# Instance normalisation on one core: units of 24 channels in 48 KB rows instead of 16 channels in 32 KB rows

## The chip, the cores and the metric

The kernel runs on one core of one Trainium2 chip. Times are device microseconds (us) of a whole run, and the metric is the median of several runs. A profile shows one execution; its span reaches from the first to the last instruction.

## The reference

The input x has shape 4 x 8 x 16 x 256 x 256 in 32-bit floats: 512 channels of 65,536 values, 134.2 MB. Each channel is normalised by itself and scaled by its gamma:

```python
mu = x.mean(axis=(3, 4), keepdims=True)
var = ((x - mu) ** 2).mean(axis=(3, 4), keepdims=True)
x_norm = (x - mu) / np.sqrt(var + 1e-5)
out = x_norm * gamma[None, :, :, None, None]
```

Gamma has 128 values and repeats for each of the four batches. Every value must be read once and written once: 268.4 MB over the memory.

## The kernel before, in words

Channels lie one after another in memory. The kernel takes them in 32 units of 16 channels. A unit is 4 MB and lies on 128 partitions with 8,192 floats (32 KB) in each, so a channel has exactly 8 whole partitions. Six slots in on-chip memory (`xt0` to `xt5`) hold six units, and unit u uses slot u mod 6.

Loads are issued ahead: the first six before the loop (units 1 and 3 on ScalarE's queue, the others on SyncE's), then, at the end of each turn of the loop, the load of unit u + 6 on SyncE's queue (L48 in `load`). That load must wait until the store of unit u has left the slot. All stores are issued by ScalarE (L139). Two small transfers go out from GpSimd at the start: `touch` (L54), a few zeros into the first unit of the output, written over later, and the gamma row (L55).

The loop runs over the 32 units. For one unit:

- VectorE sums each partition (L106), and ScalarE squares the same data and sums the squares (L107; the squares themselves go to `junk` and are not used). The two pairs of numbers stand in `st`.
- TensorE multiplies `st` with a constant matrix `navg` (L115) that adds the 8 partitions of each channel and spreads the sum back over the same 8 partitions, times minus one over 65,536. The result `ps` holds minus the mean and minus the mean square on every partition.
- VectorE forms minus the variance, `nvar` (L116), ScalarE takes the root (L120), VectorE the reciprocal (L124) and the product with gamma (L126).
- VectorE adds and multiplies the unit in place (L135). For unit 0 alone ScalarE does the last three eighths of each row (L132), with a `shift` from L131.
- ScalarE issues the store, and SyncE the load of unit u + 6.

The order on each engine is that of the program, since the schedule is written by hand (`manual_schedule`). Gamma is brought into columns before the loop: VectorE repeats it (L80), TensorE turns it into columns with eight products (L85), and VectorE copies them out (L91). An instruction of the loop that waits holds up all later ones of its engine: a store on ScalarE waits for the normalising, and the next squares stand behind it.

Of the kernel before, what the change touches and what calls it, by code (L numbers as in the profile page):

```python
# [1 line left out]

# [4 lines left out]

F32 = mybir.dt.float32
U8 = mybir.dt.uint8
ALU = mybir.AluOpType  # L10
ACTF = mybir.ActivationFunctionType
AX = mybir.AxisListType


@with_exitstack
def kernel(
    ctx: ExitStack,
    tc: tile.TileContext,
    x: bass.AP,
    gamma: bass.AP,  # L20
    out: bass.AP,
):
    nc = tc.nc
    B, G, C, H, W = x.shape
    P = nc.NUM_PARTITIONS
    HW = H * W
    n_ch = B * G * C
    S = 8
    K = P // S
    F = HW // S  # L30
    U = n_ch // K
    NG = (G * C) // K
    AHEAD = 6
    assert HW % S == 0 and (G * C) % K == 0

    xv = x.rearrange("b g c h w -> (b g c h w)").rearrange("(u p f) -> u p f", p=P, f=F)
    ov = out.rearrange("b g c h w -> (b g c h w)").rearrange("(u p f) -> u p f", p=P, f=F)
    gv = gamma.rearrange("g c -> (g c)")

    data = ctx.enter_context(tc.tile_pool(name="data", bufs=1))  # L40
    singles = ctx.enter_context(tc.tile_pool(name="singles", bufs=1))
    psum = ctx.enter_context(tc.tile_pool(name="psum", bufs=4, space=bass.MemoryType.PSUM))
    ctx.enter_context(tc.manual_schedule())

    slots = [data.tile([P, F], F32, name=f"xt{i}") for i in range(AHEAD)]

    def load(u, queue):
        queue.dma_start(out=slots[u % AHEAD][:], in_=xv[u])  # L48


    g_row = singles.tile([1, G * C], F32, name="g_row")
    touch = singles.tile([16, 128], F32, name="touch")
    nc.vector.memset(touch[:], 0.0)  # L53
    nc.gpsimd.dma_start(out=ov[0][0::S, 0:128], in_=touch[:])  # L54
# [8 lines left out]
    navg = singles.tile([P, K, S], F32, name="navg")  # L63
    nc.gpsimd.memset(navg[:], -1.0 / HW)  # L64
    nc.gpsimd.affine_select(  # L65
        out=navg[:], in_=navg[:], pattern=[[-S, K], [0, S]], compare_op=ALU.is_ge,
        fill=0.0, base=0, channel_multiplier=1,
    )
    nc.gpsimd.affine_select(  # L69
        out=navg[:], in_=navg[:], pattern=[[S, K], [0, S]], compare_op=ALU.is_ge,  # L70
        fill=0.0, base=S - 1, channel_multiplier=-1,
    )
    navg_w = navg[:].rearrange("p k s -> p (k s)")
    root_eps = singles.tile([P, 1], F32, name="root_eps")
    nc.scalar.activation(out=root_eps[:], in_=eps_t[:], func=ACTF.Sqrt)  # L75
    g_rep = singles.tile([1, NG, K, S], F32, name="g_rep")
    g_ps = psum.tile([P, NG], F32, name="g_ps", bufs=1)
    g_col = singles.tile([P, NG], F32, name="g_col")

    nc.vector.tensor_copy(  # L80
        out=g_rep[:],
        in_=g_row[:].rearrange("o (n k) -> o n k", n=NG).unsqueeze(3).to_broadcast([1, NG, K, S]),
    )
    for n in range(NG):
        nc.tensor.matmul(  # L85
            out=g_ps[:, n : n + 1],
            lhsT=g_rep[:, n].rearrange("o k s -> o (k s)"),
            rhs=one[:],
            start=True, stop=True,
        )  # L90
    nc.vector.tensor_copy(out=g_col[:], in_=g_ps[:])  # L91

    junk = singles.tile([P, F], U8, name="junk")

    st = singles.tile([P, U, 2], F32, name="st")
# [3 lines left out]
    scale = singles.tile([P, U], F32, name="scale")  # L99

    shift = singles.tile([P, 1], F32, name="shift")

    squares = []
    for u in range(U):
        t = slots[u % AHEAD]
        nc.vector.reduce_sum(out=st[:, u, 0:1], in_=t[:], axis=AX.X)  # L106
        square = nc.scalar.activation(  # L107
            out=junk[:], in_=t[:], func=ACTF.Square, accum_out=st[:, u, 1:2],
        )
        if u:  # L110

            tc.declare_no_dep(square.ins, squares[-1].ins, reason="junk, ordered by the root between")
        squares.append(square)
        ps = psum.tile([P, 2], F32, name="ps")
        nc.tensor.matmul(out=ps[:], lhsT=navg_w, rhs=st[:, u], start=True, stop=True)  # L115
        nc.vector.tensor_scalar(  # L116
            out=nvar[:, u : u + 1], in0=ps[:, 0:1], scalar1=ps[:, 0:1],
            scalar2=ps[:, 1:2], op0=ALU.mult, op1=ALU.add,
        )
        nc.scalar.activation(  # L120
            out=std[:, u : u + 1], in_=nvar[:, u : u + 1], func=ACTF.Sqrt,
            bias=eps_t[:], scale=-1.0,
        )
        nc.vector.reciprocal(out=rstd[:, u : u + 1], in_=std[:, u : u + 1])  # L124
        g = u % NG
        nc.vector.tensor_mul(  # L126
            out=scale[:, u : u + 1], in0=rstd[:, u : u + 1], in1=g_col[:, g : g + 1],
        )
        cut = F * 5 // 8 if u == 0 else F
        if cut < F:  # L130
            nc.vector.tensor_mul(out=shift[:], in0=ps[:, 0:1], in1=scale[:, u : u + 1])  # L131
            nc.scalar.activation(  # L132
                out=t[:, cut:], in_=t[:, cut:], func=ACTF.Identity, bias=shift[:], scale=scale[:, u : u + 1],
            )
        nc.vector.tensor_scalar(  # L135
            out=t[:, :cut], in0=t[:, :cut], scalar1=ps[:, 0:1], scalar2=scale[:, u : u + 1],
            op0=ALU.add, op1=ALU.mult,
        )
# [6 lines left out]
_INS = ['x', 'gamma']  # L145
_OUTS = [((4, 8, 16, 256, 256), 'float32')]


# [23 lines left out]
```

## Time and profile before

| what | value |
|---|---|
| median of 3 runs | 626.75 us (626.69 to 626.85) |
| span of the profiled execution | 625.2 us |
| busy: VectorE, ScalarE, TensorE | 441.8 us (71%), 241.8 (39%), 21.4 (3%) |
| mean DMA rate over the span | 429 GB/s |
| DMA packets | 9282, of them 8192 rows of 32 KB |
| SyncE's queue (q1), ScalarE's queue (q10) | 125.83 MB, 142.61 MB |
| memory read, written | 134.22 MB, 134.23 MB |
| time from issue to landing, median: stores, SyncE's loads | 62.5 us, 38.5 us |

The page gives no time of the profiled execution other than its span; the median of the runs is 1.5 us above it. In the tables of groups, a row has the line, the engine, the operation, what it writes and reads with shapes, the count, then the busy time in us and the mean of one in ns, and last the idle time of the engine just before these instructions with what ended it. The row of slices cuts the span into 40 equal parts; each digit is the busy share in tenths. "SPq" is SyncE's sequencer, which issues transfers and waits for semaphores. A time from issue to landing contains the time in which a transfer stands behind earlier ones of its queue.

### The profile page before, as it was taken

The numbers are of one execution on the slowest core, as the hardware profiler recorded it, in microseconds if no ns is written. First come the engines' busy times: TensorE is split into PE (matmuls) and PEld (weight loads), VectorE is DVE, ScalarE is ACT, GpSimd is POOL, SyncE is SP. The second block draws the span as 40 slices with busy tenths as digits, with TensorE's granted clock in tenths as the row PEclk, the third lists the DMA queues.
The fourth block names the chain that finished last, engine by engine and source line by source line (L and its number), as shares of the span: only waits on it lengthen the run. The fifth ranks groups of instructions, "written<-read, shape, count | busy, mean of one in ns | idle before, by whom it ended". The sixth has DMA issues, their size and how long they took to land.

```text
span 625.2 us, 635 instructions
## 1 busy us (share of the span) xinstructions
PE 21.4 (3%) x80; PEld 19.5 (3%) x80; DVE 441.8 (71%) x164; ACT 241.8 (39%) x99; POOL 2.4 (0%) x11
## 2 busy tenths in 40 slices
PE   0200000000000000000000000000000000000000
PEld 0200000000000000000000000000000000000000
DVE  0589999998776687666786767867668676687730
ACT  0464444444443244432344423444224442244400
POOL 1000000000000000000000000000000000000000
DMA  8999999999999999999999999999999999999998
GB/s 370 436 407 432 436 436 436 436 436 430 423 436 434 434 428 434 434 436 436 436 436 428 426 436 436 432 430 434 434 436 436 436 436 421 432 436 434 434 430 367
DMA packets 9282, 268.46 MB, mean 429 GB/s; under 512 B 1072, under 2 KB 1088, under 8 KB 1088
## 3 DMA queue, kind: packets, MB, share of 16 engines
q10 hardware_dynamic: 4896, 142.61, 52.9%
q1 hardware_dynamic: 4320, 125.83, 46.8%
q0 software_dynamic: 64, 0.01, 0.0%
q14 instruction: 2, 0.02, 0.0%
HBM read 134.22 MB, written 134.23 MB: 429 GB/s over the span
## 4 chain that ended last, share of the span: by engine, by line
another core or an unknown queue 61%; DMA 17%; DVE 15%; SPq 1%; PE 1%; issue 0%; ACT 0%
DMA xt<-in_x_dram 10%; DVE st L106 10%; DMA out_dram<-xt 8%; DVE xt L135 5%; SPq L48 1%; PE ps L115 1%; ACT std L120 0%; DVE nvar L116 0%; DVE rstd L124 0%; DVE scale L126 0%; DVE shift L131 0%
## 5 line engine op out<-in xcount | busy, mean ns | idle before, releaser
L106 DVE TENSOR_REDUCE st<-xt 128x1 f32<-128x8192 f32 x32 | 277.9, 8684 | 102.2 <-DMA xt<-in_x_dram 102.2
L107 ACT ACTIVATE junk<-xt 128x8192 uint8<-128x8192 f32 x32 | 225.0, 7030 | 272.0 <-DMA xt<-in_x_dram 233.8
L135 DVE TENSOR_SCALAR xt<-xt,ps,scale 128x8192 f32<-128x8192 f32 (+1 forms) x32 | 144.0, 4500 | 1.1
L120 ACT ACTIVATE std<-nvar,eps_t 128x1 f32<-128x1 f32 x32 | 9.4, 295 | 79.4 <-DVE nvar L116 79.4
L115 PE MATMUL ps<-st,navg 128*128 128x2 f32 x64 | 17.8, 348 | 557.3 <-DVE st L106 557.3
L115 PEld LDWEIGHTS ps<-st,navg 128*128 128x128 f32 x64 | 16.0, 310 | 559.1 <-issue 546.2
L116 DVE TENSOR_SCALAR nvar<-ps 128x1 f32<-128x1 f32 x32 | 9.2, 286 | 23.8 <-PE ps L115 23.8
L124 DVE RECIPROCAL rstd<-std 128x1 f32<-128x1 f32 x32 | 5.2, 163 | 11.6 <-ACT std L120 11.6
L80 DVE COPY g_rep<-g_row 1x1024 f32<-1x1024 f32 x1 | 0.7, 681 | 14.4 <-DMA g_row<-in_gamma_dram 14.4
L107 ACT ACTIVATION_READ_ACCUMULATOR junk<-xt 128x1 f32 x32 | 6.0, 186 | 0.0
L126 DVE TENSOR_TENSOR scale<-rstd,g_col 128x1 f32<-128x1 f32 x32 | 5.1, 158 | 1.1
L85 PE MATMUL g_ps<-one,g_rep 1*128 1x1 f32 x16 | 3.5, 347 | 16.3 <-DVE g_rep L80 16.3
L85 PEld LDWEIGHTS g_ps<-one,g_rep 1*128 1x128 f32 x16 | 3.5, 326 | 16.3 <-issue 16.3
L132 ACT ACTIVATE xt<-xt,shift,scale 128x3072 f32<-128x3072 f32 x1 | 2.9, 2947 | 0.7 <-DVE shift L131 0.7
L91 DVE COPY g_col<-g_ps 128x8 f32<-128x8 f32 x1 | 0.2, 167 | 3.7 <-PE g_ps L85 3.7
L75 ACT ACT_TABLE_LOAD x1 | 1.3, 1283 | 1.7 <-PEq L156 1.7
L53 DVE MEMSET touch<- 16x128 f32 x1 | 0.2, 165 | 0.9 <-PEq L156 0.9
L54 POOL DMA_DIRECT2D out_dram<-touch x1 | 0.6, 617 | 0.8 <-DVE touch L53 0.8
L55 POOL DMA_DIRECT2D g_row<-in_gamma_dram x1 | 0.5, 487 | 0.0
L65 POOL TENSOR_SCALAR_AFFINE_SELECT navg<-navg 128x128 f32<-128x128 f32 x1 | 0.4, 400 | 0.1
L69 POOL TENSOR_SCALAR_AFFINE_SELECT navg<-navg 128x128 f32<-128x128 f32 x1 | 0.4, 399 | 0.1
L64 POOL MEMSET navg<- 128x128 f32 x1 | 0.2, 230 | 0.0
(8 smaller groups left out, 1.0 us busy)
## 6 DMA issues: line engine op xcount, KB each, us to landing
out_dram<-xt ACTq DMA_DIRECT2D x32, 4096.0 KB, 62.5
xt<-in_x_dram SPq DMA_DIRECT2D x30, 4096.0 KB, 38.5
xt<-in_x_dram ACTq DMA_DIRECT2D x2, 4096.0 KB, 31.7
out_dram<-touch POOLq DMA_DIRECT2D x1, 8.0 KB, 9.3
g_row<-in_gamma_dram POOLq DMA_DIRECT2D x1, 0.5 KB, 13.5
```

The source lines that it names most:

```text
L48: queue.dma_start(out=slots[u % AHEAD][:], in_=xv[u])
L75: nc.scalar.activation(out=root_eps[:], in_=eps_t[:], func=ACTF.Sqrt)
L85: nc.tensor.matmul(out=g_ps[:, n : n + 1], lhsT=g_rep[:, n].rearrange("o k s -> o (k s)"), rhs=one[:], start=True, stop=True,)
L106: nc.vector.reduce_sum(out=st[:, u, 0:1], in_=t[:], axis=AX.X)
L107: square = nc.scalar.activation(out=junk[:], in_=t[:], func=ACTF.Square, accum_out=st[:, u, 1:2],)
L115: nc.tensor.matmul(out=ps[:], lhsT=navg_w, rhs=st[:, u], start=True, stop=True)
L116: nc.vector.tensor_scalar(out=nvar[:, u : u + 1], in0=ps[:, 0:1], scalar1=ps[:, 0:1], scalar2=ps[:, 1:2], op0=ALU.mult, op1=ALU.add,)
L120: nc.scalar.activation(out=std[:, u : u + 1], in_=nvar[:, u : u + 1], func=ACTF.Sqrt, bias=eps_t[:], scale=-1.0,)
L124: nc.vector.reciprocal(out=rstd[:, u : u + 1], in_=std[:, u : u + 1])
L126: nc.vector.tensor_mul(out=scale[:, u : u + 1], in0=rstd[:, u : u + 1], in1=g_col[:, g : g + 1],)
L132: nc.scalar.activation(out=t[:, cut:], in_=t[:, cut:], func=ACTF.Identity, bias=shift[:], scale=scale[:, u : u + 1],)
L135: nc.vector.tensor_scalar(out=t[:, :cut], in0=t[:, :cut], scalar1=ps[:, 0:1], scalar2=scale[:, u : u + 1], op0=ALU.add, op1=ALU.mult,)
```

## The change

The channels are cut into 20 units of 24 channels (6 MB, 12,288 floats or 48 KB in each partition) and, last, two units of 16 channels as before. Four slots of 48 KB a partition take the place of six of 32 KB. All loads are issued by SyncE, each as one transfer; `split` is empty. With 24 channels on 128 partitions, a channel is 16 pieces of 4,096 floats and a partition holds three pieces (j = 0, 1, 2), which can belong to two channels. So:

- the sum of a unit has three results a partition, and the squares are three instructions of 4,096;
- three products with `navg3` add up the pieces into one row for each of the 24 channels (`ps` on 24 partitions), and `nvar`, root, reciprocal and gamma are worked out on 24 partitions;
- minus the mean is copied beside the scale into `coef`, and three products with `spread` bring both back to 128 partitions, once for each piece (`wide`, in PSUM);
- VectorE normalises the three pieces one by one with both numbers read from `wide`. In units 0, 19, 20 and 21 (`helped`) ScalarE takes a part: the third piece of a 24-channel unit, or three eighths of a 16-channel one.

GpSimd makes three constant matrices instead of one. Gamma's columns come from 18 products instead of eight. `ps` and `wide` have two buffers each in PSUM, where `ps` had four.

```diff
-    S = 8
-    K = P // S
-    F = HW // S
-    U = n_ch // K
-    NG = (G * C) // K
-    AHEAD = 6
+    GC = G * C
+    F = 4096
+    SLOTS = 4
+    sizes = [2] * 0 + [3] * ((n_ch - 16 * 2) // 24) + [2] * 2
+    U = len(sizes)
+    starts = [sum(sizes[:i]) for i in range(U)]
+    split = {}
+    helped = (0, U - 3, U - 2, U - 1)
...
-    psum = ctx.enter_context(tc.tile_pool(name="psum", bufs=4, space=bass.MemoryType.PSUM))
+    psum = ctx.enter_context(tc.tile_pool(name="psum", bufs=2, space=bass.MemoryType.PSUM))
...
-    slots = [data.tile([P, F], F32, name=f"xt{i}") for i in range(AHEAD)]
-    def load(u, queue):
-        queue.dma_start(out=slots[u % AHEAD][:], in_=xv[u])
+    slots = [data.tile([P, 3 * F], F32, name=f"xt{i}") for i in range(SLOTS)]
+    def load(u):
+        cut = split.get(u, 0) * F
+        if cut:
+            nc.scalar.dma_start(out=home(u)[:, :cut], in_=rows(xf, u)[:, :cut])
+        if cut < sizes[u] * F:
+            nc.sync.dma_start(out=home(u)[:, cut:], in_=rows(xf, u)[:, cut:])
...
-    for u in range(AHEAD):
-        load(u, nc.scalar if u in (1, 3) else nc.sync)
+    for u in range(SLOTS):
+        load(u)
...
+    firsts = sorted({8 * starts[u] % GC for u in range(U) if sizes[u] == 3})
+    for n, c in enumerate(firsts):
+        nc.tensor.matmul(
+            out=g_ps3[:, n : n + 1], lhsT=g_two[:, c : c + K], rhs=one[:],
+            start=True, stop=True,
+        )
+    nc.vector.tensor_copy(out=g_col3[:], in_=g_ps3[:])
...
-        nc.vector.reduce_sum(out=st[:, u, 0:1], in_=t[:], axis=AX.X)
-        square = nc.scalar.activation(
-            out=junk[:], in_=t[:], func=ACTF.Square, accum_out=st[:, u, 1:2],
-        )
+        if three:
+            nc.vector.reduce_sum(
+                out=st[:, u, :, 0], in_=t.rearrange("p (j f) -> p j f", j=3), axis=AX.X,
+            )
...
+        step = F if three else cols
+        for j in range(cols // step):
+            square = nc.scalar.activation(
+                out=junk[:, :step], in_=t[:, j * step : (j + 1) * step],
+                func=ACTF.Square, accum_out=st[:, u, j, 1:2],
+            )
...
+            for j in range(3):
+                nc.tensor.matmul(
+                    out=ps[:n], lhsT=navg3[:, j], rhs=st[:, u, j], start=j == 0, stop=j == 2,
+                )
...
+        if three:
+            nc.vector.tensor_copy(out=coef[:n, u, 0:1], in_=ps[:n, 0:1])
...
+            for j in range(3):
+                nc.tensor.matmul(
+                    out=wide[:, j], lhsT=spread[:, j], rhs=coef[:n, u], start=True, stop=True,
+                )
+            mine = 2 if u in helped else 3
+            if u in helped:
+                own = singles.tile([P, 2], F32, name=f"own{u}")
+                nc.vector.tensor_copy(out=own[:, 1:2], in_=wide[:, 2, 1:2])
+                nc.vector.tensor_mul(out=own[:, 0:1], in0=wide[:, 2, 0:1], in1=own[:, 1:2])
+                nc.scalar.activation(
+                    out=t[:, 2 * F :], in_=t[:, 2 * F :], func=ACTF.Identity,
+                    bias=own[:, 0:1], scale=own[:, 1:2],
+                )
+            for j in range(mine):
+                nc.vector.tensor_scalar(
+                    out=t[:, j * F : (j + 1) * F], in0=t[:, j * F : (j + 1) * F],
+                    scalar1=wide[:, j, 0:1], scalar2=wide[:, j, 1:2], op0=ALU.add, op1=ALU.mult,
+                )
...
-        cut = F * 5 // 8 if u == 0 else F
+            cut = cols * 5 // 8 if u in helped else cols
...
-        nc.scalar.dma_start(out=ov[u], in_=t[:])
-        if u + AHEAD < U:
-            load(u + AHEAD, nc.sync)
+        nc.scalar.dma_start(out=rows(of, u), in_=t)
+        if u + SLOTS < U:
+            load(u + SLOTS)
```

More of the change, by code (lines that the diff above doesn't have):

```diff
@@ L38, with rows @@
+    U = len(sizes)
+    starts = [sum(sizes[:i]) for i in range(U)]
+    assert 8 * sum(sizes) == n_ch
+    split = {}
+    helped = (0, U - 3, U - 2, U - 1)
+    xf = x.rearrange("b g c h w -> (b g c h w)")
+    of = out.rearrange("b g c h w -> (b g c h w)")
     gv = gamma.rearrange("g c -> (g c)")
+    def rows(flat, u):
+        lo = starts[u] * P * F
+        return flat[lo : lo + sizes[u] * P * F].rearrange("(p f) -> p f", p=P)
     data = ctx.enter_context(tc.tile_pool(name="data", bufs=1))
@@ L52, with home @@
+    def home(u):
+        return slots[u % SLOTS][:, : sizes[u] * F]
+    def load(u):
[4 more added lines that the diff above has]
+            nc.sync.dma_start(out=home(u)[:, cut:], in_=rows(xf, u)[:, cut:])
+    g_row = singles.tile([1, GC], F32, name="g_row")
     touch = singles.tile([16, 128], F32, name="touch")
     nc.vector.memset(touch[:], 0.0)
-    nc.gpsimd.dma_start(out=ov[0][0::S, 0:128], in_=touch[:])
+    nc.gpsimd.dma_start(out=rows(of, 0)[0::8, 0:128], in_=touch[:])
@@ new lines @@
+    nc.gpsimd.affine_select(
+        out=navg3[:], in_=navg3[:], pattern=[[-1, 3], [16, K]], compare_op=ALU.is_ge,
+        fill=0.0, base=15, channel_multiplier=-3,
+    )
+    spread = singles.tile([K, 3, P], F32, name="spread")
+    nc.gpsimd.memset(spread[:], 1.0)
+    nc.gpsimd.affine_select(
+        out=spread[:], in_=spread[:], pattern=[[1, 3], [3, P]], compare_op=ALU.is_ge,
+        fill=0.0, base=0, channel_multiplier=-16,
+    )
+    nc.gpsimd.affine_select(
+        out=spread[:], in_=spread[:], pattern=[[-1, 3], [-3, P]], compare_op=ALU.is_ge,
+        fill=0.0, base=15, channel_multiplier=16,
+    )
@@ L74 @@
     root_eps = singles.tile([P, 1], F32, name="root_eps")
     nc.scalar.activation(out=root_eps[:], in_=eps_t[:], func=ACTF.Sqrt)
[L76 to L82, printed above, removed]
-    )
-    for n in range(NG):
+    g_two = singles.tile([1, GC + K], F32, name="g_two")
@@ new lines @@
+    nc.vector.tensor_copy(out=g_two[:, :GC], in_=g_row[:])
+    nc.vector.tensor_copy(out=g_two[:, GC:], in_=g_row[:, :K])
+    sixteens = sorted({8 * starts[u] % GC for u in range(U) if sizes[u] == 2})
+    g_rep = singles.tile([1, len(sixteens), 16, 8], F32, name="g_rep")
+    g_ps = psum.tile([P, len(sixteens)], F32, name="g_ps", bufs=1)
+    g_col = singles.tile([P, len(sixteens)], F32, name="g_col")
+    for n, c in enumerate(sixteens):
+        nc.vector.tensor_copy(
+            out=g_rep[:, n], in_=g_row[:, c : c + 16].unsqueeze(2).to_broadcast([1, 16, 8]),
+        )
@@ L85 @@
         nc.tensor.matmul(
-            out=g_ps[:, n : n + 1],
-            lhsT=g_rep[:, n].rearrange("o k s -> o (k s)"),
-            rhs=one[:],
+            out=g_ps[:, n : n + 1], lhsT=g_rep[:, n].rearrange("o k s -> o (k s)"), rhs=one[:],
             start=True, stop=True,
@@ L98 @@
     rstd = singles.tile([P, U], F32, name="rstd")
-    scale = singles.tile([P, U], F32, name="scale")
+    coef = singles.tile([P, U, 2], F32, name="coef")
     shift = singles.tile([P, 1], F32, name="shift")
@@ L104 @@
     for u in range(U):
-        t = slots[u % AHEAD]
-        nc.vector.reduce_sum(out=st[:, u, 0:1], in_=t[:], axis=AX.X)
-        square = nc.scalar.activation(
-            out=junk[:], in_=t[:], func=ACTF.Square, accum_out=st[:, u, 1:2],
[L109 to L113, printed above, removed]
-        ps = psum.tile([P, 2], F32, name="ps")
-        nc.tensor.matmul(out=ps[:], lhsT=navg_w, rhs=st[:, u], start=True, stop=True)
+        t = home(u)
@@ new lines @@
+        three = sizes[u] == 3
+        cols = sizes[u] * F
+        if three:
+            nc.vector.reduce_sum(
+                out=st[:, u, :, 0], in_=t.rearrange("p (j f) -> p j f", j=3), axis=AX.X,
+            )
+        else:
+            nc.vector.reduce_sum(out=st[:, u, 0, 0:1], in_=t, axis=AX.X)
+        step = F if three else cols
[3 more added lines that the diff above has]
+                func=ACTF.Square, accum_out=st[:, u, j, 1:2],
+            )
+            if squares and j == 0:
+                tc.declare_no_dep(square.ins, squares[-1].ins, reason="junk, ordered by the root between")
+            squares.append(square)
@@ L116 @@
+        n = K if three else P
+        ps = psum.tile([P, 2], F32, name="ps")
+        if three:
+            for j in range(3):
+                nc.tensor.matmul(
+                    out=ps[:n], lhsT=navg3[:, j], rhs=st[:, u, j], start=j == 0, stop=j == 2,
+                )
+        else:
+            nc.tensor.matmul(
+                out=ps[:], lhsT=navg2[:].rearrange("p k s -> p (k s)"), rhs=st[:, u, 0],
+                start=True, stop=True,
+            )
         nc.vector.tensor_scalar(
-            out=nvar[:, u : u + 1], in0=ps[:, 0:1], scalar1=ps[:, 0:1],
@@ L118 @@
-            scalar2=ps[:, 1:2], op0=ALU.mult, op1=ALU.add,
+            out=nvar[:n, u : u + 1], in0=ps[:n, 0:1], scalar1=ps[:n, 0:1],
+            scalar2=ps[:n, 1:2], op0=ALU.mult, op1=ALU.add,
         )
         nc.scalar.activation(
-            out=std[:, u : u + 1], in_=nvar[:, u : u + 1], func=ACTF.Sqrt,
-            bias=eps_t[:], scale=-1.0,
-        )
[L124 to L128, printed above, removed]
@@ L140 @@
-        if u + AHEAD < U:
-            load(u + AHEAD, nc.sync)
+            out=std[:n, u : u + 1], in_=nvar[:n, u : u + 1], func=ACTF.Sqrt,
+            bias=eps_t[:n], scale=-1.0,
+        )
+        if three:
+            nc.vector.tensor_copy(out=coef[:n, u, 0:1], in_=ps[:n, 0:1])
+        nc.vector.reciprocal(out=rstd[:n, u : u + 1], in_=std[:n, u : u + 1])
+        if three:
+            g = firsts.index(8 * starts[u] % GC)
+            gamma_u = g_col3[:, g : g + 1]
+        else:
+            g = sixteens.index(8 * starts[u] % GC)
+            gamma_u = g_col[:, g : g + 1]
```

55 lines of the change are left out of this document (34 added, 21 removed).

## The prediction

> **What bounds the kernel now.** I read the page's slices first, then its queues, its groups of instructions, the queue engine's waits and the chain of waits, and last the two ends of the span in half-microsecond windows. The slices, DMA share and rate:
>
> ```profile
> DMA  8999999999999999999999999999999999999998
> GB/s 370 436 407 432 436 436 436 436 436 430 423 436 434 434 428 434 434 436 436 436 436 428 426 436 436 432 430 434 434 436 436 436 436 421 432 436 434 434 430 367
> ```
>
> The 16 DMA engines are full in every slice but the first and last. No compute engine is (VectorE, the busiest, 71%):
>
> ```profile
> L106 DVE TENSOR_REDUCE st<-xt 128x1 f32<-128x8192 f32 x32 | 277.9, 8684 | 102.2 <-DMA xt<-in_x_dram 102.2
> L107 ACT ACTIVATE junk<-xt 128x8192 uint8<-128x8192 f32 x32 | 225.0, 7030 | 272.0 <-DMA xt<-in_x_dram 233.8
> L135 DVE TENSOR_SCALAR xt<-xt,ps,scale 128x8192 f32<-128x8192 f32 (+1 forms) x32 | 144.0, 4500 | 1.1
> ```
>
> The reduction and the squares wait for loads, never for each other for long. And loads wait for stores to leave a slot, as SyncE's own waits say:
>
> ```profile
> SPq L48 <- DMA out_dram<-xt: 514.7, 26, 39.7
> ```
>
> The chain of waits (start, length, what) gives the beat of one unit:
>
> ```profile
> 159.94 0.33 SPq L48
> ...
> 179.27 0.33 SPq L48
> ...
> 547.02 0.03 issue
> ```
>
> The load issued at 159.94 and the one issued at 547.05 (at the end of the last row) are 20 units apart: 387.1 / 20 = 19.356 us a unit, for one load and one store of 4.194 MB, 433.4 GB/s. Thirty-two units are 619.4. The rest of the span stands at its ends (last columns: DMA share, GB/s; a packet counts where it starts):
>
> ```profile
> 1.00:1.50 0.50, 0.00 (x0) 0.00 (x0) 0.06 (x1) 0.00 (x0) 0.14 (x1) 1.00 0.00 0
> 1.50:2.00 0.50, 0.00 (x0) 0.00 (x0) 0.00 (x0) 0.27 (x1) 0.50 (x2) 1.00 1.83 524
> ...
> 622.50:623.00 0.50, 0.00 (x0) 0.00 (x0) 0.00 (x0) 0.00 (x0) 0.00 (x0) 1.00 0.15 66
> 623.00:623.50 0.50, 0.00 (x0) 0.00 (x0) 0.00 (x0) 0.00 (x0) 0.00 (x0) 1.00 0.01 0
> ```
>
> In the trace's packet records the first row starts at 1.82 and the last ends at 623.93. So the span of 625.2 is 1.8 + 622.1 of DMA + 1.3. Of the 622.1, 619.4 is the beat and 2.7 irregular: the first packets took 1.25 to 2.01 us instead of 1.213 (0.65 lost), those around 41 us, where the first store joins, up to 2.01 (0.75), and the rest is small change and the engines' uneven finish. The median of the runs is 626.75, 1.5 over the span; I carry that 1.5 over.
>
> So only three things can move the time: what a packet costs beyond its bytes, when the engines have nothing to move, and the two ends.
>
> **Packets.** In the packet records a 512 B packet of touch took 27 ns and a 32 KB row 1213 ns: (32768 - 512) / (1213 - 27) = 27.2 bytes a ns. Sixteen rows (8 in, 8 out, per engine) are 16 x 32768 / 27.2 = 19.276 us; the beat of 19.356 leaves 0.080 us a unit for 16 packets and two 4-byte completions, 2.56 us in all. After: 40 transfers of 8 x 48 KB rows and four of 8 x 32 KB per engine, so 352 packets and 44 completions instead of 512 and 64. Both ratios are 0.6875: 2.56 becomes 1.76, **0.8 us saved**. If the residue is a clock and not a cost per packet, 0; if a 48 KB row goes out as three 16 KB packets (1024 of them), 2.56 more. I take 0.8: 512 B and 32 KB lie on one line whose intercept is some 8 ns, so the residue is per packet.
>
> **Head.** Before, SyncE and ScalarE's queue each issue loads at 0.81; after, SyncE alone issues four (before, its four issues took 0.38 to 0.61 us each and were done by 2.8). First packet at 1.82 as before. One 6 MB load alone is 8 x 1.81 = 14.5 us, so loads last until 1.8 + 0.65 + 58 = 60.5 if nothing joins. From here to the first store one queue is alone. Before never shows loads alone; both bounds come from rows: stores alone, after 604, ran 32 KB rows at the same 1.209 spacing (nothing lost), and the first packets, with nothing ahead, lost 0.65. Some 24 packets an engine at 0.65 would be 15.6 us. I take 0: the second packet of each engine in the head is already down to 1.21 to 1.27. The Trainium skill weighs both ways. Its page DMA: Bandwidth & Descriptors, section Issuing engines are not separate DMA queues, says all queues run on the same 16 engines, so a second one saves only issue time: by that, 0. But its section iDMA fabric gives 408.7 GB/s for one load stream from SP alone (4 KiB rows); an estimate from that figure over 44 us, against 433.4, is 2.7 us lost. No run here shows it yet.
>
> Then the store of unit 0 must be there before loads run out, and the store of unit 1 before store 0 ends. Unit 0: lands at 1.8 + 0.65 + 14.5 + 1.6 (the lag from last packet to reduction, 583.99 to 585.57) = 18.5. VectorE first waits for gamma: its row landed at 15.5 behind four turns of two 1.21 us packets, now of one 1.81 (11 to 15.5); four small copies, about 1; then 18 matmuls instead of 8 (8 took 3.54: 8.0), whose second eviction stands ahead of reduction 0 in VectorE's order. So it starts at 20 to 24.5. Each unit: reduction 12288 / 8192 x 8.68 = 13.0; meanwhile three squares at 3.76 (line through 7.03 at 8192 and 2.95 at 3072 of L132) plus 0.19 to read out, 11.8, hidden by 1 us; three matmuls 1.7 at most (0.57 each, L115); nvar, root, reciprocal, product and the copy of the mean, 1.1 (0.29, 0.30, 0.16, 0.16 and gaps; the copy is beside the root); three spreading matmuls 1.7; three normalising pieces of 2.4 (line through 4.55 at 8192 and 2.94 at 5120), 7.2. Sum 24.8. For a helped unit ScalarE's third (3.8) lies beside two pieces (4.8) after 0.3 for own: 22.7. From 24.5: store 0 is ready at 47.2, store 1 at 72.0, 73.0 with 1.0 from issue to packet. The engines have four loads and store 0: 1.8 + 1.4 + 72.5 = 75.7. **Covered by 2.7 us** at the worst start, 7 at the best. Load 4 waits for store 0 on SyncE, with later loads queued behind it; store 1 runs alone meanwhile. PSUM's two buffers instead of four, and GpSimd's six more constants (0.2 to 0.4 each in the rows), end long before use: 0.
>
> **Middle.** The beat of a 6 MB unit is 8 x 2 x 1.811 = 29.0 us; VectorE needs 24.8 (86%). A slot is held for a load 29, the chain 24.8 and a store 29: 83 of 4 x 29 = 116, so loads keep 16 us and stores about 17 of slack. ScalarE's stores stand behind 13 us of squares and root; its issue is 0.34. All hidden: 0.
>
> **Tail.** With 32 KB loads against 48 KB stores alternating, load 21 ends near 590. Its chain: 1.6 + 8.7 + 1.8 + 0.2 + 2.95 = 15.3, plus 1.0: 606.5. Stores 19 and 20 keep the engines until 614. Eight us of cover: 0 for the helping of the last three units, which only widens it. The last completion lag stays 1.3.
>
> **Sum:** 625.2 - 0.8 = 624.4 span, **625.9** as a run's median.
>
> **Rivals**, with chances (0.2% or 1.25 us is about what a measurement here can tell from no change).
> - The forecast, 0.56: 625.9, own range 625.2 to 626.8 (packet saving 0 to 0.9, irregular 2.7 a little up or down; 0.10 of the 0.56 falls under 625.5).
> - The irregular time goes too, 0.14: with one queue there is no change of two queues at 41 us, 0.9 less in 20 to 45: 625.0. Against it: store 0 still joins somewhere.
> - The lone load queue leaves gaps, 0.12: place, the first 45 us; price, 24 packets times the gap; slower than before by over 0.2% from a gap of 0.085 us ((1.25 + 0.8) / 24). At the full 0.65, 641; at a tenth, 627.5. For it: first packets at 2.0. Against: the spacing of stores alone. On the Trainium skill's figure above, 628.6.
> - Store 1 comes late, 0.08: the engines stop at 75.7 until it is there, a us for a us beyond 73.0 + 2.7. Gamma or the spreading chain 6 us longer than worked out gives 629.
> - VectorE becomes the bound, 0.04: if pieces scaled from PSUM run at the reduction's 1.06 ns an element, 13.0 in place of 7.2 makes a unit 30.6 against 29.0; 24.5 + 20 x 30.6 + 45 for the last two units and the last store gives about 680. Against: L135 already reads one PSUM scalar at 0.55.
> - The change doesn't do what it says, 0.06: rows are cut into 16 KB packets, 626.75 + 2.56 = 629.3.
>
> Faster: 0.10 + 0.14 = 0.24. Slower: 0.08 of the lone queue, 0.06 of the late store, 0.04 and 0.06, 0.24. Same: 0.52. **Range** 624.8 to 629.4, which holds the forecast, the second case, the cut rows and the mild half of the queue and store cases.
>
> **What would show it.** Right: DMA at 9 in all inner slices, about 6,500 packets (9282 - 160 x 16 rows - 20 x 16 completions = 6402), a beat of 29.0, first and last packet at 1.8 and 623. The lone queue: under 420 GB/s from 5 to 45. The late store: a hole after 75. VectorE bound: its busy share near 9 and loads waited for by nobody. Cut rows: over 9,000 packets. Wrong if any chain step here is mis-sized by over 3 us before 73, or loads alone run below stores alone.

## The result, and the profile after

The changed kernel takes **630.77 us** (median of 5 runs, 629.82 to 631.64) against 626.75 before: a ratio of 1.0063, with a 95% interval of 1.0051 to 1.0075. It is slower by 4.0 us, where 0.8 faster was forecast. Measured again later, it took 629.61 (627.87 to 631.78) against 626.87 for the kernel before, run beside it. So it also scatters over 4 us, which the kernel before, at 626.6 to 627.7 in all runs, does not. Runs more than 1.5% above the fastest of the same kernel count as slow and are left out of the medians below; there are two, both of one experiment.

The profiled execution took 629.82, with a span of 628.0 against 625.2. Its page, in the order of the prediction: slices, packets, instruction queues.

```profile
DMA  9999999999999999999999999999999999999996
GB/s 389 416 398 451 429 423 451 426 426 448 426 429 446 429 426 448 429 426 445 432 426 445 432 426 445 426 430 445 426 429 448 426 429 448 418 432 441 429 425 288
DMA packets 6405, 268.50 MB, mean 428 GB/s; under 512 B 752, under 2 KB 768, under 8 KB 768
...
q8 instruction: 2, 0.03, 0.0%
q14 instruction: 3, 0.02, 0.0%
```

6,405 packets: 6,402 were forecast and the other three are instruction packets, so a 48 KB row is one packet. The engines are full to the last slice, which has fallen from 367 to 288 GB/s. New are two packets of instructions on q8, 16 KB each. In the page before only q14 stands:

```profile
q14 instruction: 2, 0.02, 0.0%
```

The groups and SyncE's waits, then two issues of loads from the chain of waits:

```profile
L168 ACT ACTIVATE junk<-xt 128x4096 uint8<-128x4096 f32 (+1 forms) x62 | 231.1, 3728 | 290.1 <-DMA xt<-in_x_dram 268.7
L161 DVE TENSOR_REDUCE st<-xt 128x3 f32<-128x12288 f32 x20 | 259.1, 12953 | 95.1 <-DMA xt<-in_x_dram 95.1
L221 DVE TENSOR_SCALAR xt<-xt,wide 128x4096 f32<-128x4096 f32 x58 | 137.1, 2420 | 28.6 <-PE wide L208 28.6
```

```profile
SPq L66 <- DMA out_dram<-xt: 539.3, 18, 55.0
```

```profile
220.08 0.33 SPq L66
...
539.02 0.33 SPq L66
```

Compute still waits for loads, and loads for stores. The two issues are 11 units apart: 318.94 / 11 = 28.995 us. Before, 6 MB took 1.5 x 19.356 = 29.034. **The beat is shorter, as forecast.** The loss is at the end (windows of 1 us of the changed kernel; the last two columns are DMA share and GB/s):

```profile
621.00:622.00 1.00, 0.00 (x0) 0.00 (x0) 0.00 (x0) 0.00 (x0) 0.00 (x0) 1.00 1.22 524
622.00:623.00 1.00, 0.00 (x0) 0.00 (x0) 0.00 (x0) 0.00 (x0) 0.00 (x0) 1.00 0.38 164
623.00:624.00 1.00, 0.00 (x0) 0.00 (x0) 0.00 (x0) 0.00 (x0) 0.00 (x0) 1.00 0.08 33
624.00:625.00 1.00, 0.00 (x0) 0.00 (x0) 0.00 (x0) 0.00 (x0) 0.00 (x0) 1.00 0.23 98
625.00:626.00 1.00, 0.00 (x0) 0.00 (x0) 0.00 (x0) 0.00 (x0) 0.00 (x0) 1.00 0.08 33
```

A share of 0.08 is one 32 KB row (1.21 us on one of 16 engines). From 623 on, one to three engines still start rows and the others are done. The packet records say the same. The middle engine's last store is complete at 623.0 (before: 623.4), but the last engine ends at 626.5 (before: 623.9). A transfer is complete when all 16 engines are, so **one engine that is behind sets the end.**

From the packet records one can follow that engine, since its next row starts where the last one ends; followed so, each of the 16 engines comes out with 176 load rows and 176 store rows. On its first row and when store 0 joined it lost 2.4 us against rows in the middle, the others 1.7 to 2.5. The mean over the engines is 2.1; in the kernel before it is 1.4. It lost 1.42 at 417.7 to 420.5, where one of the q8 packets (0.97 us) stands between its rows, and 1.2 in three single rows right after a store's completion packet (508, 537 and 588 us). Another 0.5 went in the 570s. It never stood idle before its last row ended. The other q8 packet, at 189 us, cost a second engine 1.42 (it ends at 625.6). A third late engine, which ends at 625.4, carries no instruction packet: it lost 2.5 us in the first rows and at the joining, and 2.4 in single rows later.

### The profile page after: what moved, and what is told of

It reads as the page before. It is cut to its first block, busy times and chain, and to the rows that moved or that the text cites. A ratio compares the mean times of both kernels' runs of the same rounds, so it can differ in the third digit from the quotient of the medians.

```text
span 628.0 us, 1084 instructions
## 1 busy us (share of the span) xinstructions
PE 39.1 (6%) x280; PEld 36.6 (6%) x280; DVE 434.8 (69%) x181; ACT 258.4 (41%) x152; POOL 4.4 (1%) x17
## 2 busy tenths in 40 slices
DMA packets 6405, 268.50 MB, mean 428 GB/s; under 512 B 752, under 2 KB 768, under 8 KB 768
## 4 chain that ended last, share of the span: by engine, by line
another core or an unknown queue 68%; DMA 16%; DVE 11%; PE 1%; SPq 1%; ACT 1%; issue 0%; ACTq 0%
DMA xt<-in_x_dram 8%; DMA out_dram<-xt 7%; DVE st L161 6%; DVE xt L221 3%; DVE st L165 1%; SPq L66 1%; PE wide L208 1%; ACT xt L229 0%; ACT std L191 0%; PE ps L179 0%; DVE nvar L187 0%; DVE rstd L197 0%; DVE coef L204 0%; PE ps L183 0%
## 5 line engine op out<-in xcount | busy, mean ns | idle before, releaser
L168 ACT ACTIVATE junk<-xt 128x4096 uint8<-128x4096 f32 (+1 forms) x62 | 231.1, 3728 | 290.1 <-DMA xt<-in_x_dram 268.7
L161 DVE TENSOR_REDUCE st<-xt 128x3 f32<-128x12288 f32 x20 | 259.1, 12953 | 95.1 <-DMA xt<-in_x_dram 95.1
L221 DVE TENSOR_SCALAR xt<-xt,wide 128x4096 f32<-128x4096 f32 x58 | 137.1, 2420 | 28.6 <-PE wide L208 28.6
L179 PE MATMUL ps<-st,navg 128*24 128x2 f32 x120 | 7.4, 178 | 490.3 <-DVE st L161 490.3
L208 PE MATMUL wide<-coef,spread 24*128 24x2 f32 x120 | 28.2, 347 | 23.0 <-DVE coef L204 23.0
L208 PEld LDWEIGHTS wide<-coef,spread 24*128 24x128 f32 x120 | 27.0, 321 | 24.1 <-issue 23.0
L165 DVE TENSOR_REDUCE st<-xt 128x1 f32<-128x8192 f32 x2 | 17.4, 8686 | 14.9 <-DMA xt<-in_x_dram 14.9
L216 ACT ACTIVATE xt<-xt,own 128x4096 f32<-128x4096 f32 x2 | 7.6, 3802 | 4.8 <-DVE own L215 4.8
L183 PE MATMUL ps<-st,navg 128*128 128x2 f32 x4 | 1.1, 348 | 41.8 <-DVE st L165 41.8
L183 PEld LDWEIGHTS ps<-st,navg 128*128 128x128 f32 x4 | 1.0, 311 | 41.9 <-issue 41.9
```

What stands on the lines that cost most here:

```text
L161: nc.vector.reduce_sum(out=st[:, u, :, 0], in_=t.rearrange("p (j f) -> p j f", j=3), axis=AX.X,)
L165: nc.vector.reduce_sum(out=st[:, u, 0, 0:1], in_=t, axis=AX.X)
L168: square = nc.scalar.activation(out=junk[:, :step], in_=t[:, j * step : (j + 1) * step], func=ACTF.Square, accum_out=st[:, u, j, 1:2],)
L179: nc.tensor.matmul(out=ps[:n], lhsT=navg3[:, j], rhs=st[:, u, j], start=j == 0, stop=j == 2,)
L208: nc.tensor.matmul(out=wide[:, j], lhsT=spread[:, j], rhs=coef[:n, u], start=True, stop=True,)
L216: nc.scalar.activation(out=t[:, 2 * F :], in_=t[:, 2 * F :], func=ACTF.Identity, bias=own[:, 0:1], scale=own[:, 1:2],)
```

## The experiments

All medians are compared with runs of the kernel before on the same chip (626.87 to 627.11 there).

**Theories.** A: TensorE's many more instructions are fetched over the same DMA engines, 16 KB at a time on one engine, and that engine ends late. Rivals: B, 48 KB rows cost by themselves; C, the lone load queue costs at the start; D, the last store is issued too late (612.15 in the profile, where a few engines run dry for 0.1 to 0.4 us at about 612.8). Later P: joining a lone load queue sets engines out of step.

### Fewer products in the changed kernel, more in the kernel before

```diff
-            for j in range(3):
-                nc.tensor.matmul(
-                    out=ps[:n], lhsT=navg3[:, j], rhs=st[:, u, j], start=j == 0, stop=j == 2,
-                )
+            nc.tensor.matmul(out=ps[:n], lhsT=navg3[:, 0], rhs=st[:, u, 0], start=True, stop=True)
```

> The changed kernel with one third of TensorE's products: per 24-channel unit one product with navg3 and one with spread instead of three each (the other pieces' sums are left out, and piece 0's numbers are used for all three pieces), and six gamma products instead of 16. Transfers, VectorE's and ScalarE's work in the loop stay. Theory A (instruction fetches: the two 16 KB packets on the instruction queue q8 at 189 and 419 us each held one DMA engine 1.4 us, and the slowest of 16 engines ends the run): no q8 packet in the middle, or one, last packet near 624 to 625 instead of 626.5, median 627 to 628.5 instead of 630.8. Theory B (48 KB rows by themselves make the engines drift apart): 630 to 631.5. Theory C (one load queue alone at the start costs 0.6): 630 to 631. Theory D (the last store is issued too late): under 0.5 faster, since the chain of unit 21 does not change.

Measured: 628.93 (628.68 to 630.15), 2.0 over the kernel before. One q8 packet was left, at 477 us, and the engine that carries it ends last, at 625.5. But the middle engine ends at 624.4, 1.4 later than in the changed kernel: by the packet records most engines have rows here that take 0.1 to 0.6 us longer, mostly load rows behind a store row. What does that to this kernel stays open, and with it what the missing products are worth.

```diff
         nc.tensor.matmul(out=ps[:], lhsT=navg_w, rhs=st[:, u], start=True, stop=True)
+        for _ in range(3):
+            nc.tensor.matmul(out=dump[:], lhsT=navg_w, rhs=st[:, u], start=True, stop=True)
```

> The kernel before with three more products per unit into a spare PSUM tile that nobody reads: 544 product and weight-load instructions instead of 160, near the 560 of the changed kernel. Nothing else changes. Theory A: two q8 packets of 16 KB fall into the run, each some 1.4 us on one engine, so the last packet ends near 624.5 to 626 instead of 623.9 and the median is 627.3 to 629. Theories B, C, D: 626.7 to 626.9.

Measured: **627.76** (627.42 to 627.99; ratio 1.0013, 1.0004 to 1.0021), 0.85 over the kernel before. Its page has the two packets, which the page of before lacks:

```profile
q8 instruction: 2, 0.03, 0.0%
```

They stand at 307.6 and 561.3 us and each cost one engine 1.34 us; the last engine, which carries the first of them, ends at 624.7. Products that nobody waits for cost time through the DMA engines. A holds, at the low end of its range.

### The change without its rows, and with two load queues

```diff
-    SLOTS = 4
-    sizes = [2] * 0 + [3] * ((n_ch - 16 * 2) // 24) + [2] * 2
+    SLOTS = 6
+    sizes = [2] * 32
```

> The changed kernel with 32 units of 16 channels in 32 KB rows and six slots, all loads on SyncE's queue, the last three units helped, two PSUM buffers: all of the change but the 48 KB rows with what they need. Theory A: TensorE has as few instructions as before, so 626.5 to 627.5. Theory B: the same. Theory C: 627.3 to 627.8, the 0.6 of the start and no drift. Theory D: 626.5 to 626.9.

Measured: 628.13 (627.82 to 629.49; ratio 1.0023, 1.0013 to 1.0034), 1.2 over. Without the 48 KB rows, and with as few products as before, something is still lost. In the profiled one a q8 packet at 608.6 made one engine late (624.4); in the kernel before it comes at 625.6, after the last store. But the last engine (624.6) carries no such packet, only one of 8 KB.

```diff
-    split = {}
+    split = {1: 3, 3: 3}
```

> The changed kernel with the loads of units 1 and 3 on ScalarE's queue. Theory A and B: as the changed kernel, 630 to 631.5. Theory C: 0.5 to 1 faster, 629.8 to 630.3, the first packets and the joining of store 0 losing 1.5 in place of 2.1 together. Theory D: as the changed kernel.

Measured: 631.25 (630.82 to 638.34). C as stated falls. Here loads 0 and 1 share the engines, so unit 0 lands late. In the profiled execution, the slowest, the engines stand idle for 1.3 us in the mean at 76, before store 1 (issued at 76.82): the late store of the prediction's rivals, in another kernel.

### No spread, the queue alone, and transfers alone

```diff
-                    out=ps[:n], lhsT=navg3[:, j], rhs=st[:, u, j], start=j == 0, stop=j == 2,
+                out=ps[:], lhsT=navg2[:].rearrange("p k s -> p (k s)"), rhs=st[:, u, 0],
...
-            wide = psum.tile([P, 3, 2], F32, name="wide")
...
-                    scalar1=wide[:, j, 0:1], scalar2=wide[:, j, 1:2], op0=ALU.add, op1=ALU.mult,
+                    scalar1=ps[:, 0:1], scalar2=coef[:, u, 1:2], op0=ALU.add, op1=ALU.mult,
```

> The changed kernel without the spread: per 24-channel unit one product with the 16-channel matrix on 128 partitions, no copy to 24 partitions and back, one gamma column for all (the channel sums and scales are those of piece 0 and of the wrong partition groups). TensorE then runs about 100 products and weight loads each way instead of 560, fewer than in the kernel before. All 48 KB transfers stay. Theory A (instruction fetches and the slowest engine): no q8 packet before the end, last packet near 624, all engines done within 1.5 us of each other, median 627.5 to 628.5. Theory B (48 KB rows): 629 to 631. Remaining over the kernel before, by the fewer-products run: 1 to 1.5 from the head and the joining of the first store, whose lost time grows with the row.

Measured: **627.56** (627.04 to 630.21), 0.6 over the kernel before and 2 to 3 under the changed kernel. No q8 packet; the last engine ends at 623.8 in the profiled run, the fastest. The runs fall in two groups, six at 627.0 to 627.6 and five at 628.7 to 630.2.

```diff
-        load(u, nc.scalar if u in (1, 3) else nc.sync)
+        load(u, nc.sync)
```

> The kernel before with all six first loads on SyncE's queue. Theory C (a lone load queue leaves gaps): 627.3 to 628.1, as the run with small units (628.1 against 626.9). Theory A: 626.8 to 627.1, since there the q8 packet at 608 us, ahead of the end, made the difference.

Measured: **630.24** (627.77 to 631.82; ratio 1.0050, 1.0032 to 1.0068), the surprise of the set. One line that moves two of 32 loads to the other queue costs the kernel before 3.3 us, with 32 KB rows and no q8 packet before the last store. The rate in its middle is that of the kernel before, and its end again that of stragglers:

```profile
300.00:400.00 100.00, 2.79 (x10) 2.51 (x10) 70.48 (x26) 37.09 (x15) 0.00 (x0) 1.00 1.00 433
500.00:600.00 100.00, 2.79 (x10) 2.51 (x10) 70.60 (x26) 38.45 (x16) 0.00 (x0) 1.00 1.00 433
623.00:624.00 1.00, 0.00 (x0) 0.00 (x0) 0.00 (x0) 0.00 (x0) 0.00 (x0) 1.00 1.22 524
624.00:625.00 1.00, 0.00 (x0) 0.00 (x0) 0.00 (x0) 0.00 (x0) 0.00 (x0) 1.00 0.16 66
625.00:626.00 1.00, 0.00 (x0) 0.00 (x0) 0.00 (x0) 0.00 (x0) 0.00 (x0) 1.00 0.08 33
626.00:627.00 1.00, 0.00 (x0) 0.00 (x0) 0.00 (x0) 0.00 (x0) 0.00 (x0) 1.00 0.15 66
```

By the packet records the first and last engine to complete a load are 0.5 us apart at unit 0, 1.5 at unit 3 and 4.3 at unit 31. In each unit some two engines have one row of 1.3 to 1.7 us in place of 1.213, in 29 of 53 cases the load row right after a store's completion packet. The price is not that of the queue alone: the kernel with small units above has the same loads on the same queue, issues its first store at 28.6 us (here 28.9), and loses 1.2.

The next two kernels have no arithmetic; the loop holds the transfers alone, and they copy the input to the output.

```diff
     for u in range(U):
         t = home(u)
-        three = sizes[u] == 3
...
         nc.scalar.dma_start(out=rows(of, u), in_=t)
```

> Transfers alone: 32 units of 4 MB in 32 KB rows, six slots, loads on SyncE's queue, stores on ScalarE's as soon as a load has landed; no arithmetic, the input is copied to the output. Reference for the next run. All theories: the packet sum, 619.4 + 1.8 + 1.3 and about 2 irregular in the span, 624 to 625.5, a median of 625.5 to 627.

Measured: **626.98** (626.69 to 628.02). The kernel before, at 626.93, costs no more than its transfers. All loads are on SyncE's queue here too, and nothing is lost.

> The same with 20 units of 6 MB in 48 KB rows, two of 4 MB, four slots. Packet sum of the prediction: 0.8 less than the run with 32 KB rows, or 0.3 to 0.8 less with the longer start and joining. Theory A: 0.3 to 0.8 faster than it, no engine more than 1.5 us behind. Theory B: 1 to 3 us slower than it, engines 2 to 3 us apart at the end although no instruction fetch fell on one.

Measured: **627.61** (626.88 to 629.35), 0.6 over the run with 32 KB rows. The intervals of the two ratios to the kernel before overlap (1.0004 to 1.0021 and 0.9993 to 1.0010), but the 0.8 saved is not there. The middle engine ends at 623.85, not 623.4: first rows and joining took 2.1 us instead of 1.7, and at 613 most engines stand idle for 0.1 to 1.3 us, until the last store comes. So this is not B's drift of engines, and that the no-spread kernel (627.56), in which no engine stands idle, has nearly the same time is no proof of the same loss.

### How loads and stores meet

```diff
-    split = {}
+    split = {0: 1, 1: 1, 2: 1}
```

> The changed kernel with the loads of units 0, 1 and 2 split: the first third of each row on ScalarE's queue, the rest on SyncE's. Landing times stay, both queues are busy from the first packet, and store 0 joins behind loads that end together on both queues at about 46, with load 3 beside it. Theory P (when store 0 joins a lone load queue, some engines fall out of step with the rest and drift by 1 to 4 us; loads all on SyncE cost the kernel before 3.3): 628.5 to 630 and engines under 3 us apart at the end. Theory A (TensorE's instruction fetches alone): as the changed kernel, 630 to 631.5.

Measured: 635.78 (633.4 to 639.24).

The same line in the kernel without the spread:

> The same split of the first three loads in the kernel without the spread (sums and scales of piece 0 only, as in that run). Theories A and P together: both losses gone, the packet saving shows, 626.0 to 626.9, and runs agree within 0.5. Theory A alone: 627.3 to 627.8, as without the split. Theory B (48 KB rows cost by themselves): 627.3 to 628.

Measured: 636.58 (632.47 to 640.08). Both are far outside every theory. By the packet records, store 0 and load 3 now run side by side, each ending at about 79.5, and all engines' rows are stretched between 50 and 90 us, in sum by 4.1 and 4.4 us an engine in the mean (2.2 to 6.0). The two profiled runs are 12.1 and 5.6 us over the kernel before, so that is a part of it.

```diff
-        load(u, nc.scalar if u in (1, 3) else nc.sync)
+        load(u, nc.scalar if u == 1 else nc.sync)
```

> The kernel before with unit 3's load on SyncE's queue, so that ScalarE's queue carries unit 1 alone and is empty from about 22 us until store 0 joins at about 37. Theory P (joining a lone queue sets engines out of step): 627.5 to 630, with runs over 1 us apart. Lead (loads that run ahead of the first store give the last store its cover; store 0 joins 6 us earlier here, so the last store is issued some 3 us later than 600.6, still ahead of 613): 626.8 to 627.1.

Measured: 627.02 (626.94 to 628.62), 0.15 over and within noise. A lone load queue that a store joins is not enough: P as stated falls.

> The changed kernel itself, for comparison on the same chip and beside the same runs of the kernel before: 630 to 631.5.

Measured: 629.61 (627.87 to 631.78). The fastest, 627.87, is the profiled one: both q8 packets are there, and its last engine ends at 624.3.

### How much is fetches, and is the last store late?

```diff
+            for _ in range(5):
+                nc.tensor.matmul(
+                    out=dump[:], lhsT=navg2[:].rearrange("p k s -> p (k s)"), rhs=st[:, u, 0],
+                    start=True, stop=True,
+                )
```

> The kernel without the spread, plus five products per 24-channel unit into a spare PSUM tile that nobody reads, so that TensorE again runs as many instructions as the changed kernel (about 490 products and weight loads instead of 100). Chain, transfers and everything else as without the spread (sums and scales of piece 0 only). Theory A (fetches): one or two q8 packets in the run, 628.3 to 630.5, at least 0.8 over the run without the spread beside it. If it was the shorter chain without the spread that helped: the same as that run within 0.4.

> The kernel without the spread again, for comparison on the same chip: 627.2 to 628.2.

Measured side by side: 628.67 (627.86 to 630.6) with the idle products and 627.66 (627.2 to 628.94) without, 1.0 more with the chain unchanged. But a run's time less its span is 2.3 us with the idle products and 1.8 without (medians), so half of the 1.0 lies outside the span, where no transfer of the loop runs. The spans are 626.3 and 625.9, with ranges that overlap (625.5 to 628.7, 625.4 to 627.1). **That the fetches cost the transfers 1.0 us here is not shown.** In the profiled run with the idle products the engine that carries the second of two q8 packets is the last to end, at 624.8; without them the last ends at 624.2.

```diff
+        if u == U - 1:
+            cut = sizes[u] * F * 5 // 8
+            nc.scalar.activation(
+                out=t[:, cut:], in_=t[:, cut:], func=ACTF.Identity,
+                bias=shift[:], scale=coef[:, u - 1, 1:2],
+            )
...
+            nc.scalar.dma_start(out=rows(of, u), in_=t)
+            continue
```

> The changed kernel, in which the last unit is scaled with the numbers of the unit before it as soon as it has landed (its own sums, root and products are left out), so that the last store is issued some 10 us earlier. Theory D (the last store is late and the engines wait for it): 0.5 to 1.5 faster than the changed kernel, 628.5 to 629.5, and no dip of the rate at 612. Theory A and drift of single engines: under 0.4 faster, 629.5 to 630.8, since the slowest engine has work of its own until the end.

Measured: 629.93 (627.57 to 631.92). The last store is issued at 601.71, 10.4 us earlier:

```profile
601.71 0.34 ACTq L168 DMA_DIRECT2D out_dram<-xt  x1
```

The time stays within the changed kernel's scatter (629.61 and 630.77), which is too wide to exclude a gain of some tenths. The traces say more: in the changed kernel's profile the engine that ends last never waits for the last store, so D is not what sets the end. In this run the two engines with a q8 packet end at 622.8 and 624.1, and the last one, at 626.6, carries none: an engine can be as late as that without a fetch.

The same in the kernel before with all loads on SyncE's queue:

```diff
+        if u == U - 1:
+            nc.vector.tensor_scalar(
+                out=t[:], in0=t[:], scalar1=shift[:], scalar2=scale[:, u - 1 : u],
+                op0=ALU.add, op1=ALU.mult,
+            )
```

> The kernel before with all loads on SyncE's queue, and the last unit scaled as soon as it has landed with the numbers of the unit before it and no shift worth the name (its sums are left out). Theory D: most of the 3.3 lost by the queue comes back, 626.8 to 628. Drift of single engines: 629 to 630.5, with engines 3 to 4 us apart at the end.

Measured: 629.92 (627.35 to 635.5, ten runs; two more took 637.16 and 645.2). The last store is issued at 605.44 instead of 613.69, and the median does not come back to D's 626.8 to 628. In the run without this edit 13 engines do stand idle at 613, for 0.4 to 1.5 us, but not the last three to end.

### Only the first store's time is changed

```diff
...
+    for j, w in enumerate((12288, 12288)):
+        nc.scalar.activation(
+            out=junk[:, :w], in_=home(0)[:, :w], func=ACTF.Square, accum_out=st[:, j : j + 1],
+        )
     for u in range(U):
```

> Transfers alone in 32 KB rows, all loads on SyncE's queue, but two squares on ScalarE hold the first store until about 29 us, as late as in the kernel before with all loads on SyncE's queue (28.9); every later store still follows its load. If the first store's late joining of a lone load queue is enough to send single engines adrift: 628 to 631, with runs over 1 us apart. If it takes the engines' work beside it (reductions, squares, roots in step with the transfers): 626.8 to 627.3.

Measured: **644.93** (643.7 to 645.48; ratio 1.028).

> The same in 48 KB rows with two squares before the first store, which is issued near 40 us, as in the changed kernel (39.7). Late joining enough: 628.5 to 631. Not enough: as the transfers alone with 48 KB rows, 627.3 to 628.

Measured: **726.21** (724.67 to 730.64; ratio 1.160, 1.157 to 1.162). The aim was missed: a store issue does not wait for the square before it to end (the second square ran from 28.83 to 39.27), so the first store left at 28.8 us instead of 18.7 (48 KB) and at 20.3 instead of 13.1 (32 KB), not at 40 and 29. The two do not copy the moments of the kernels with arithmetic, then. But a shift of 7 to 10 us alone does far more than any theory had it. The 48 KB transfers with an early first store, in windows of 100 us:

```profile
100.00:200.00 100.00, 0.00 (x0) 0.00 (x0) 1.00 1.01 435
200.00:300.00 100.00, 0.00 (x0) 0.00 (x0) 1.00 1.01 435
```

And with a late one (DVE, ACT, POOL, clock, DMA share, GB/s):

```profile
100.00:200.00 100.00, 0.00 (x0) 0.00 (x0) 0.00 (x0) 1.00 1.00 376
200.00:300.00 100.00, 0.00 (x0) 0.00 (x0) 0.00 (x0) 1.00 0.99 371
```

The share is 1.0 in both: the engines are as busy, but rows take longer. By the packet records rows of 1.815 us become 1.9 to 3.4. Here store j runs beside load j + 2, and on the middle engine both end together (both at 65.6, 99.8, ... 473.1). With the early store, load j + 1 ends 8 us ahead of store j, and rows keep 1.815. So **the first store's time sets how long rows take for the rest of the run**. That it does so through which load rows run beside which store rows fits these traces, but no run changes the one without the other.

## Why the prediction was wrong, point by point

- **The step that failed: the irregular time.** The sum carried over the kernel before's 2.7 us between the beat and the DMA time ("a little up or down") and let the end lie where one engine's packets put it. In the changed kernel's profile the DMA time is 626.5 - 1.8 = 624.7 us and the beat gives 20 x 28.995 + 2 x 19.33 = 618.6, so 6.1 are irregular, 3.4 more. Nearly all of it is one engine's delay: the last engine ends 3.5 us after the middle one, in the kernel before 0.5. Middle and tail were worked out for one engine, and the packet saving (0.8) is smaller than what one of 16 can fall behind.
- **A term left at nothing: fetches.** The prediction counts the added products as time in the chain (1.7 us for three) and nowhere else; their instructions also take time on the DMA engines that fetch them. One fetch of 16 KB costs its engine 1.3 to 1.4 us, and the idle products in the kernel before cost 0.85.
- **Packets: right.** 6,405 packets, beat 28.995 against 29.034, the middle engine's last store done at 623.0 against 623.4. That is about half of the 0.8; the first rows and the joining took 0.7 us more in the mean (2.1 instead of 1.4), a size that the prediction left as it was.
- **Head: the sum was right, the reach was not.** It priced the lone load queue by gaps between rows and took 0. There are none: load 0 ends at 17.3 and load 1 at 31.8, so 6.29 MB took 14.5 us as worked out, 434 GB/s; from 5 to 35 us, before store 0, the changed kernel's windows of 10 us give 409, 457 and 413 GB/s. The Trainium skill's 408.7 (page DMA: Bandwidth & Descriptors, section iDMA fabric) was measured with 4 KiB rows; with 48 KB rows this trace is above it. But the queue change also moves the point at which stores join the loads. In the kernel before, the same change alone cost 3.3 us (630.24 against 626.93), at the end of the run; the kernel with small units, on the same queue, lost 1.2 in all, and the transfers alone nothing. The other sentence weighed there (section Issuing engines are not separate DMA queues), that a second queue saves issue time only, does not hold for the kernel before with both loads moved. How much of the changed kernel's loss is due to its one load queue is not shown: two queues there took 631.25, with unit 0 landing late.
- **Chain times: on the safe side.** Reduction 12.95 (13.0 forecast), squares 3.62, pieces 2.42. The 24-column products are cheaper than the 128-column ones they were bounded by: six in 0.37 us, and the 32 for gamma in 1.44. So gamma was ready before unit 0 landed, and store 0 was issued at 39.7, not at 42.7 to 47.2. By the prediction's own sign (a chain step off by over 3 us before 73) that is a miss: the first store's time, which the last two runs show to matter, was 3.0 to 7.5 us off.
- **Tail: cover gone, at no cost that shows.** The last store was issued at 612.15 instead of 605.5, since load 21 is done when the slowest engine is (596 instead of 590). Issuing it 10 us earlier changed nothing beyond the scatter.
- **Rivals.** The irregular time grew where one rival had it go; no gap in the head, no hole at 75, VectorE at 69%, rows uncut: none of the five happened.

How the 2.7 to 4.0 us split is known in part. What a fetch does to its engine is shown; how much later the run ends by it depends on how late that engine is anyway. In the changed kernel's fastest run (627.87, 1.0 over the kernel before) the last engine is one with a q8 packet, and after 60 us it lost nothing else. The rest, up to 3 us and different from run to run, stands in single stretched rows of a few engines, mostly right after store completions. What stretches them stays open. That the first store's time can stretch rows is shown for transfers alone; in the changed kernel store 0 is complete on the middle engine at 72.7 and load 3 at 80.3, in the no-spread kernel at 71.0 and 81.8, so they meet nearly alike there, and it loses 0.6. Taking out the spread takes away 2 to 3 us; it takes out products, their fetches and a piece of the chain together, and the runs do not say which of these counts. Open too is which distance and phase are bad: the kernel before runs store j beside load j + 4, ending together, and loses nothing. No version tried beats the kernel before, which is at the time of its bare transfers.

## What to carry to other kernels

When DMA is the bound and all 16 engines are full, look at when the slowest engine ends, not only at the mean rate: a change worth 0.1% in packets can be lost in one engine's delay. Added instructions on an idle engine are not always free there, since their fetches take DMA time on single engines (0.85 us of the run in the kernel before). A change of queues, slots or the first store also changes which load runs beside which store, so measure it by itself: the same transfers took 627.6 or 726.2 us.

## What the runs showed of the hardware that was not expected

- An instruction fetch of 16 KB delays one DMA engine by 1.3 to 1.4 us, one of 8 KB by 0.4 to 0.85 (packet records: 0.85 and 0.56 in the kernel before at 144 and 199 us, 0.56 and 0.42 in the changed one at 169 and 593).
- Transfers alone fall from 435 to 371 GB/s, at a DMA share of 1.0 in both, when only the first store is held back from 18.7 to 28.8 us.
- Two of 32 loads moved to the other queue cost the kernel before 3.3 us (six runs, 627.8 to 631.8); one of them, 0.15, within noise.
